# Layer 0: key squares summed with a 32-column selector as the stationary side, four token tiles in four column groups, roots on rows of tokens

## The chip, the cores and the metric

The kernel runs on one core of one Trainium2 chip, as one program launch. Its time is the device time of that core in microseconds (us). A core has five engines that work side by side, each on a queue of its own: PE (TensorE, matrix products; its weight loads are listed as PEld), DVE (VectorE), ACT (ScalarE), POOL (GpSimd) and SP (SyncE, which here issues the DMAs). They wait for one another through semaphores. Three runs of the kernel before took 1411.02, 1413.55 and 1410.15 us, a median of 1411.02 us.

## The reference, cut to what matters

The reference is one step of a streaming encoder with two layers. A layer is a norm, a projection, a token mixer beside a memory attention, a gate, an output projection and a residual. There are 512 prompt tokens and 32 sample tokens, which the kernel treats as 544 columns of one row. Layer 0 mixes tokens with RWKV-7, with 24 heads of 64 channels. The change lies in two normalisations of that mixer:

```python
kk = k * k_k.reshape(RW_HEADS, RW_HD)
kk = kk / maximum(norm(kk, axis=-1, keepdims=True), 1e-12)        # per token and head: the key norm
k  = k * (1.0 + (a - 1.0) * k_a.reshape(RW_HEADS, RW_HD))
def step(S, inp):                                                 # over the tokens
    r_t, k_t, v_t, w_t, kk_t, a_t = inp
    sa = einsum('bhvk,bhk->bhv', S, -kk_t)
    S = S * w_t[:, :, None, :] + sa[..., None] * (kk_t * a_t)[:, :, None, :] + v_t[..., None] * k_t[:, :, None, :]
    return S, einsum('bhvk,bhk->bhv', S, r_t)
S_T, y = lax.scan(step, S0, xs)
mean = mean(y, axis=-1); var = mean(square(y - mean), axis=-1)
y = (y - mean) * rsqrt(var + GN_EPS) * ln_w + ln_b                # per token and head: the output norm
y = y + sum(r * k * r_k, axis=-1, keepdims=True) * v
```

Both need a reciprocal square root for each token and head: 544 x 2 roots for a pair of heads for the keys, and as many for the outputs.

## The kernel before, in words

Layer 0 goes through 12 pairs of heads, 128 channels on the 128 partitions. What belongs to a pair is cut into kinds of work, each a Python generator whose steps are recorded one at a time by `go(kind, pr)`:

- "prep" (`rw_prep`) makes the operands of a pair from its projected rows. It squares the keys (`sq`), sums the squares over the 64 channels of a head on PE (`ps_ss`), clips the sums into `q20`, makes decays (`ps_wa`, `th`, `cum`, `de`), and later multiplies the keys by the roots: the roots are split into a high and a rest part (`rr`), transposed on PE (`ps_rt`), copied by ACT (`r4`, in the profile r<-ps_rt) and spread over the channels by a product with the selector `hs4` (`ps_b`).
- "chain" (`chunk`) is the recurrence itself, nine chunks of tokens and three hops for each: `ps_c<-SB,zr` then `avz` on DVE, `ps_c<-avz,at` then `sv` on ACT, `ps_c<-sv,bt` then `SB` on DVE. Each hop waits for the engine before it.
- "mrg" (`rw_merge`) builds the triangular inverses of a pair with small products, in two of its steps `ps_w<-t1b,at` (t1b is a transpose on DVE) and `ps_w<-at,wm`.
- "fin" (`rw_finish`) is the output norm of the pair before: mean, squares, sums into the other half of `q20`, `yt` times the root on DVE, five transposes on PE (`ps_y`), two DVE operations that read them (`bv<-ps_y`), and the gate.
- "rsq" takes the roots of all 20 columns of `q20` at once into `r20` (in the profile both are called q), by eight DVE operations on 128x20 elements, a start value from the bits and two iterations. Those on `nt` belong to it.

Token tiles lie on partitions for these roots: `ps_ss` has one column for each head and each of five token tiles, made by five products with `sq` as the stationary side and the selector `hsel` (128x2) as the moving side.

All the rest of PE's time goes to the large projections `ps_g`. Each weight block is loaded by DMA (raw) and split into a high part by ACT (`whi`) and a rest by DVE (`wlo`). One `ps_g` pass streams 272 columns. They form one endless generator, `main`, and fill every place between the small products.

The order is fixed by the program. Every PE, DVE and ACT instruction goes through `tie`, which makes it follow the one before it on its engine; therefore all of them carry line 104 in the profile (105 after the change). For each pair a table `PLAN` of 23 steps sets what is recorded: a step is one hop of the chain, then two halves, each a list of (kind, pair offset, PE us, DVE us). The last two numbers are costs by hand: `took` and `load` add them up and give each half a due time, up to which `next(main)` adds `ps_g` passes. `some(room)` puts the splits of weight blocks (`wlo`, `whi`) where DVE's sum has room. Pairs 0 to 2 are prepared ahead by `FILL0` to `FILL3` with "rsq" behind their third prep step; pair `pr` prepares pair `pr`+3 and finishes pair `pr`-1 for `pr` = 1 to 8.

Two tile pools in PSUM matter: `psm` with several buffers (tag "m"), and `psx` with one buffer:

```python
self.psx = self.pool("psx", 1, space=PS)
```

`ps_w` of "mrg", the first four transposes of `ps_y`, `ps_yc` and `ps_rt` all come from `psx`. Whoever writes there next waits until the last reader of the one before is done; for `ps_y` that is the first DVE operation `bv<-ps_y`.

Of the kernel before, what the change touches and what calls it, by code (L numbers as in the profile page):

```python
# [31 lines left out]
GN_EPS = 64e-5  # L32
KAPPA = 0.5 * math.exp(-0.5)
QB, KB = 2, 1
RKV = 4
# [13 lines left out]
    [[("val", 0, 0.95, 0), ("prep", 2, 0.1, 0)], [("prep", 2, 0, 0.42)]],  # L49
# [57 lines left out]
class Trunk:  # L107
# [20 lines left out]

    def rsqrt(self, y, x, pool, tag):

        nc = self.nc
        t = pool.tile(list(y.shape), F32, tag=tag, name=tag)
        f = 0.375 ** 0.2
        self.ve.tensor_scalar(y.bitcast(I32), x.bitcast(I32), -0.5, float(0x5F3759DF), ALU.mult, ALU.add)
        self.ve.scalar_tensor_tensor(t[:], y, -0.5 * f, y, ALU.mult, ALU.mult)
        self.ve.tensor_tensor(t[:], t[:], x, ALU.mult)
        self.ve.scalar_tensor_tensor(y, t[:], 1.5 * f, y, ALU.add, ALU.mult)
        self.ve.tensor_tensor(t[:], y, y, ALU.mult)
        self.ve.tensor_tensor(t[:], t[:], x, ALU.mult)
# [2044 lines left out]
```

## Time and profile before

| what | value |
|---|---|
| median of 3 runs | 1411.02 us (1410.15 to 1413.55) |
| the profiled execution, its span | 1409.44 us, 1407.5 us |
| PE busy | 1368.6 us, 97% of the span |
| DVE, ACT, POOL busy | 932.4, 823.9, 374.7 us (66%, 59%, 27%) |
| layer 0's pairs with prep and fin (`pr` = 1 to 8) | about 46.1 us each, from 180 us to 550 us |

A busy share says how long an engine worked, not whether the end hung on it. PE works 97% of the span, so each idle stretch of PE is short, and a row in the timeline names it and what ended it in brackets. Products on PE overlap: a `ps_g` pass is shown with 0.29 us but the next begins 0.125 us after it, so the price of a product is read from the distance of the starts. A float32 product counts as two passes, so x10 in the timeline are five `ps_ss` products, and x32 are the 16 small products of `ps_w`.

### The profile page before, as it was taken

The page shows a single profiled execution, that of the slowest core. Times are in us where ns is not written, and L with a number is a line of the kernel's source. Part 1 is how long each engine was busy: PE and PEld are TensorE (multiplying, and loading weights), DVE is VectorE, ACT ScalarE, POOL GpSimd, SP SyncE. Part 2 cuts the span into 40 slices and gives each one's busy share as a digit, 9 for nine tenths or more (in the row PEclk, how much of TensorE's full clock was granted, in tenths as well). Part 3 has the DMA queues.
Part 4 walks back from the last instruction along what each step waited for, and adds up shares of the span by engine and source line. Part 5 has one row for each costly group of instructions (what it writes and reads, how often), then busy time and mean ns, then how long its engine had stood idle before and what let it go on. Part 6 is the DMA issues. An engine that isn't in the chain of part 4 may idle for free.

```text
span 1407.5 us, 31863 instructions
## 1 busy us (share of the span) xinstructions
PE 1368.6 (97%) x11877; PEld 1304.7 (93%) x11877; DVE 932.4 (66%) x2345; ACT 823.9 (59%) x2282; POOL 374.7 (27%) x838
## 2 busy tenths in 40 slices
PE   8999999999999999999999999999999999999997
PEld 6998899999999998898899999999999999999997
DVE  5676777777877887676753466666466756667443
ACT  5765677767786777555543356664466546665222
POOL 2137558655765577510000040000000001001100
PEclk9999999999999999999999999999999999999999
DMA  7543222332233222342464473333333323332321
GB/s 222 155 118 82 61 56 65 80 98 60 67 81 94 67 73 73 95 119 77 130 182 130 131 200 104 91 92 93 98 91 93 103 73 84 93 103 89 91 76 72
DMA packets 264036, 139.45 MB, mean 99 GB/s; under 512 B 57721, under 2 KB 252802, under 8 KB 263882
## 3 DMA queue, kind: packets, MB, share of 16 engines
q1 hardware_dynamic: 263818, 137.41, 34.6%
q8 instruction: 94, 1.54, 0.5%
q14 instruction: 60, 0.49, 0.1%
q10 hardware_dynamic: 64, 0.02, 0.0%
HBM read 111.12 MB, written 22.91 MB: 95 GB/s over the span
## 4 chain that ended last, share of the span: by engine, by line
PE 78%; DVE 9%; ACT 8%; issue 2%; DMA 1%; SPq 1%; DVEq 0%; ACTq 0%
PE ps_g L104 54%; PE ps_c L104 4%; PE ps_at L104 2%; PE ps_o L104 2%; ACT pt L104 2%; PE ps_s L104 2%; DVE wlo L104 2%; PE ps_v L104 1%; ACT whi L104 1%; PE ps_mm L104 1%; PE ps_mo L104 1%; PE ps_ss L104 1%; PE ps_yc L104 1%; PE ps_w L104 1%; ACT kh L104 1%
## 5 line engine op out<-in xcount | busy, mean ns | idle before, releaser
L104 PE MATMUL ps_g<-hh,wlo 128*128 128x272 f32 x1808 | 537.2, 298 | 2.4 <-DVE wlo L104 2.4
L104 PE MATMUL ps_g<-hh,whi 128*128 128x272 f32 x1808 | 537.6, 298 | 0.4 <-DVE memk L104 0.2
L104 PE MATMUL ps_g<-hl,whi 128*128 128x272 f32 x1808 | 533.0, 296 | 0.6 <-DVE hl L104 0.3
L104 PEld LDWEIGHTS ps_g<-hh,wlo 128*128 128x128 f32 x1808 | 340.9, 189 | 8.0 <-DVE wlo L104 3.5
L104 PEld LDWEIGHTS ps_g<-hh,whi 128*128 128x128 f32 x1808 | 341.6, 189 | 5.1 <-DVE og L104 0.6
L104 PEld LDWEIGHTS ps_g<-hl,whi 128*128 128x128 f32 x1808 | 340.9, 189 | 4.7 <-DVE hl L104 1.3
L104 DVE TENSOR_TENSOR wlo<-raw,whi 128x512 fp32r<-128x512 f32 x314 | 219.0, 708 | 124.0 <-ACT whi L104 119.2
L104 ACT CAST whi<-raw 128x512 fp32r<-128x512 f32 x314 | 189.6, 617 | 108.1 <-PE ps_g L104 60.2
L851 POOL TENSOR_TENSOR tm<-u,m 102x84 f32<-102x84 f32 (+23 forms) x341 | 148.6, 436 | 165.4 <-DMA m<-sc 139.7
L853 POOL TENSOR_TENSOR u<-u,tm 102x84 f32<-102x84 f32 (+23 forms) x341 | 146.3, 429 | 26.7
L104 PE MATMUL ps_g<-hi,whi 128*128 128x272 f32 x512 | 148.9, 291 | 0.0
L104 PE MATMUL ps_g<-hi,wlo 128*128 128x272 f32 x512 | 147.8, 289 | 0.4 <-DVE wlo L104 0.4
L104 PE MATMUL ps_g<-lo,whi 128*128 128x272 f32 x512 | 147.7, 288 | 0.0
L1305 POOL TENSOR_TENSOR lo<-og,hi 128x544 fp32r<-128x544 f32 x8 | 13.2, 1648 | 462.0 <-ACT hi L104 461.5
L104 PEld LDWEIGHTS ps_g<-hi,wlo 128*128 128x128 f32 x512 | 96.4, 188 | 0.6 <-DVE wlo L104 0.6
L104 PEld LDWEIGHTS ps_g<-lo,whi 128*128 128x128 f32 x512 | 96.4, 188 | 0.0
L104 PEld LDWEIGHTS ps_g<-hi,whi 128*128 128x128 f32 x512 | 96.4, 188 | 0.0
L104 ACT ACTIVATE pt<-ps_s,snm 128x128 f32<-128x128 f32 (+3 forms) x96 | 50.9, 532 | 42.1 <-DVE snm L104 41.8
L104 DVE SCALAR_TENSOR_TENSOR SB<-ps_c,dl,sd 64x64 f32<-64x64 f32 x168 | 47.5, 283 | 42.4 <-PE ps_c L104 38.9
L1724 POOL TENSOR_TENSOR hl<-hn,hh 128x544 fp32r<-128x544 f32 x8 | 12.7, 1590 | 210.5 <-ACT hh L104 210.4
L104 ACT COPY sv<-ps_c 64x64 f32<-64x64 f32 x192 | 39.5, 206 | 44.4 <-PE ps_c L104 42.5
L104 ACT ACTIVATE sg<-ps_g 128x272 f32<-128x272 f32 x64 | 25.3, 395 | 58.1 <-PE ps_g L104 53.6
(388 smaller groups left out, 2583.2 us busy)
## 6 DMA issues: line engine op xcount, KB each, us to landing
raw<-in_rw_in_dram SPq DMA_DIRECT2D x114, 256.0 KB
raw<-in_df_in_dram SPq DMA_DIRECT2D x112, 256.0 KB
raw<-in_w_out_dram SPq DMA_DIRECT2D x64, 256.0 KB
oscr<-sg SPq DMA_DIRECT2D x16, 272.0 KB
lo<-oscr SPq DMA_DIRECT2D x16, 272.0 KB
m<-sc SPq DMA_DIRECT2D x33, 128.0 KB
raw<-in_w_mem_v_dram SPq DMA_DIRECT2D x16, 256.0 KB
kh<-kh SPq DMA_DIRECT2D x24, 136.0 KB
```

What stands on the lines that cost most here:

```text
L104: return lambda *a, **k: self.trunk.tie(self, issue(*a, **k))
L851: nc.gpsimd.tensor_tensor(tm[:, :n, :wd], u3[:, :n, kx : kx + 1].to_broadcast(sh), m3[:, kx : kx + 1, kx + 1 :].to_broadcast(sh), ALU.mult)
L853: nc.gpsimd.tensor_tensor(u3[:, :n, kx + 1 :], u3[:, :n, kx + 1 :], tm[:, :n, :wd], ALU.add)
L1305: (self.nc.gpsimd if g % 2 and self.o1 else self.ve).tensor_tensor(lo[:], t, hi[:].bitcast(F32), ALU.subtract)
L1724: nc.gpsimd.tensor_tensor(self.hl[:, k, :], h[:], self.hh[:, k, :].bitcast(F32), ALU.subtract)
```

## The change

- `hsel` becomes the stationary side with 32 columns (head 0 in the even, head 1 in the odd ones), and `sq` the moving side. Four products of 32x128 write the four token tiles of the prompt to four groups of 32 rows in PSUM (`tile_position=(0, 32 * i)`), four of 32x32 write the sample tokens beside them. The sums lie on rows of tokens now, 160 columns (`NS`), each 16 times over.
- The roots are therefore taken on 128x160 or, with the 10 columns of the output norm behind them, on 128x170 (`qn`, `r20`). `newton` has the same eight operations, and can stop in the middle: "half" in `PLAN` stands for four of them. The 10 columns are now scaled in `roots` instead of in `rw_finish`.
- `ps_rt`, its DVE inputs and its ACT copy go. `rr` is the rounded root (CAST, 128x160), and `r4` is made by one more DVE operation that leaves the root in the even row pairs and the rest in the odd ones (`nlo` is a column of 0 and -1, made once). `hs4` is built for these rows.
- `PLAN` changes in its last seven steps: "rsq" becomes two "half", and the steps of "fin" that use the roots, `yt` and `ps_y` with `bv<-ps_y`, and the gate, stand half a step to one step later. The costs by hand change too, and with them the places of the `ps_g` passes.

The diff, cut to its core (a few rows of `PLAN` and of the constants are left out):

```diff
-    [[("prep", 3, 1.04, 0.17)], [("mrg", 1, 0, 0.86)]],
-    [[("mrg", 1, 0.9, 0)], [("rsq", 0, 0, 1.5)]],
-    [[("prep", 3, 0.33, 0)], [("fin", -1, 0, 0.88)]],
-    [[("prep", 3, 0.33, 0)], [("prep", 3, 0, 0.1), ("fin", -1, 0.6, 1.0)]],
-    [[("prep", 3, 0.33, 0)], [("mrg", 1, 0.9, 0), ("prep", 3, 0.33, 0), ("fin", -1, 0, 0.73)]],
-    [[("prep", 3, 0, 1.45), ("val", 1, 0.45, 0)], [("prep", 3, 0, 0.5)]],
-    [[("out", 0, 1.6, 0.7)], [("prep", 3, 0, 0)]]]
+    [[("prep", 3, 0.52, 0.35)], [("mrg", 1, 0, 0.86)]],
+    [[("mrg", 1, 0.9, 0)], [("half", 0, 0, 1.5)]],
+    [[("prep", 3, 0.33, 0)], [("half", 0, 0, 1.4)]],
+    [[("prep", 3, 0.33, 0), ("fin", -1, 0, 0.88)], [("prep", 3, 0, 0.1)]],
+    [[("prep", 3, 0.33, 0), ("fin", -1, 0.6, 1.0)], [("mrg", 1, 0.9, 0), ("prep", 3, 0.33, 0)]],
+    [[("prep", 3, 0, 1.45), ("val", 1, 0.45, 0)], [("fin", -1, 0, 0.73), ("prep", 3, 0, 0)]],
+    [[("out", 0, 1.6, 0.7)], [("prep", 3, 0, 0.7)]]]
...
 
+    def roots(self):
+
+        c = slice(0 if self.qn is not None else NS, NS + 10 if self.gs is not None else NS)
+        if self.qn is None:
+            self.qn = self.rk0.tile([P, 2, NS + 10], F32, tag="gsq", name="qn", bufs=1)
+        q, t = self.qn[:, 0, c], self.qn[:, 1, c]
+        if self.gs is not None:
+            self.ve.tensor_scalar(self.qn[:, 0, NS:], self.gs[:], 1.0 / 64, GN_EPS, ALU.mult, ALU.add)
+        self.qn = self.gs = None
+        yield from self.newton(self.r20[:, c], q, t)
+
     def rsqrt(self, y, x, pool, tag):
 
-        nc = self.nc
-        t = pool.tile(list(y.shape), F32, tag=tag, name=tag)
+        for _ in self.newton(y, x, pool.tile(list(y.shape), F32, tag=tag, name=tag)[:]):
+            pass
+
+    def newton(self, y, x, t):
+
         f = 0.375 ** 0.2
         self.ve.tensor_scalar(y.bitcast(I32), x.bitcast(I32), -0.5, float(0x5F3759DF), ALU.mult, ALU.add)
-        self.ve.scalar_tensor_tensor(t[:], y, -0.5 * f, y, ALU.mult, ALU.mult)
-        self.ve.tensor_tensor(t[:], t[:], x, ALU.mult)
-        self.ve.scalar_tensor_tensor(y, t[:], 1.5 * f, y, ALU.add, ALU.mult)
-        self.ve.tensor_tensor(t[:], y, y, ALU.mult)
-        self.ve.tensor_tensor(t[:], t[:], x, ALU.mult)
-        self.ve.scalar_tensor_tensor(t[:], t[:], -10.0 / 3.0 * f ** 2, t[:], ALU.add, ALU.mult)
-        self.ve.scalar_tensor_tensor(y, t[:], 5.0 * f ** 4, y, ALU.add, ALU.mult)
+        self.ve.scalar_tensor_tensor(t, y, -0.5 * f, y, ALU.mult, ALU.mult)
+        self.ve.tensor_tensor(t, t, x, ALU.mult)
+        self.ve.scalar_tensor_tensor(y, t, 1.5 * f, y, ALU.add, ALU.mult)
+        yield
+        self.ve.tensor_tensor(t, y, y, ALU.mult)
+        self.ve.tensor_tensor(t, t, x, ALU.mult)
+        self.ve.scalar_tensor_tensor(t, t, -10.0 / 3.0 * f ** 2, t, ALU.add, ALU.mult)
+        self.ve.scalar_tensor_tensor(y, t, 5.0 * f ** 4, y, ALU.add, ALU.mult)
 
     def params(self, p, name, rows, queue=None):
 
...
-        self.hsel = c.tile([P, 2], F32, name="hsel")
+        self.hsel = c.tile([P, 32], F32, name="hsel")
-        nc.gpsimd.memset(self.hsel[:64, 0:1], 1.0)
-        nc.gpsimd.memset(self.hsel[64:, 1:2], 1.0)
+        nc.gpsimd.memset(self.hsel[:64, 0:32:2], 1.0)
+        nc.gpsimd.memset(self.hsel[64:, 1:32:2], 1.0)
-        self.hs4 = c.tile([P, 5, P], F32R, name="hs4")
+        self.hs4 = c.tile([P, 4, P], F32R, name="hs4")
-        self.ve.scalar_tensor_tensor(self.hs4[:], t4[:], 10.0, t5[:], ALU.is_equal, ALU.add)
+        self.ve.scalar_tensor_tensor(self.hs4[:], t4[:], 2.0, t5[:], ALU.is_equal, ALU.add)
+        self.nlo = c.tile([P, 1], F32, name="nlo")
+        self.ve.tensor_reduce(self.nlo[:], t5[:].rearrange("p i c -> p (i c)"), AX.X, ALU.max)
+        self.ve.tensor_scalar(self.nlo[:], self.nlo[:], -1.0, None, ALU.add)
...
         pss = self.psm.tile([P, 512], F32, tag="m", name="ps_ss")
-        for i in range(5):
-            c = min(i * P, T - P)
-            self.te.matmul(pss[:, 2 * i : 2 * i + 2], sq[:, c : c + P], self.hsel[:], start=True, stop=True)
-        self.ve.tensor_scalar(self.q20[:, :10], pss[:, :10], 1e-24, None, ALU.max)
+        for o, c, d in ((0, 0, P), (P, TP, 0)):
+            for i in range(4):
+                n = P if o == 0 else TS
+                self.te.matmul(pss[32 * i : 32 * i + 32, o : o + n], self.hsel[:], sq[:, c + i * d : c + i * d + n],
+                               start=True, stop=True, tile_position=(0, 32 * i))
+        self.qn = self.rk0.tile([P, 2, NS + 10], F32, tag="gsq", name="qn", bufs=1)
+        self.ve.tensor_scalar(self.qn[:, 0, :NS], pss[:, :NS], 1e-24, None, ALU.max)
...
         yield
-        rr = self.rr
-        self.ve.tensor_copy(rr[:, :10], self.r20[:, :10])
-        self.ve.tensor_tensor(rr[:, 10:20], self.r20[:, :10], rr[:, :10].bitcast(F32), ALU.subtract)
-        yield
         de = p.tile([P, CW], F32, tag="de", name="de", bufs=1)
         di = cum
         self.ae.activation(de[:, :CU], cum[:, :CU], AF.Exp, scale=-KAPPA)
         self.ae.activation(di[:, :CU], cum[:, :CU], AF.Exp, scale=KAPPA)
         yield
-        pst = self.psx.tile([P, 512], F32, tag="x", name="ps_rt")
-        self.te.transpose(pst[:, :P], rr[:].bitcast(F32), self.ident[:])
-        r4 = p.tile([P, P], F32R, tag="uh", name="r4", bufs=1)
-        self.ae.copy(r4[:], pst[:, :P])
+        rr = self.rr
+        self.ve.tensor_copy(rr[:], self.r20[:, :NS])
+        r4 = p.tile([P, NS], F32R, tag="uh", name="r4", bufs=1)
+        self.ve.scalar_tensor_tensor(r4[:], rr[:].bitcast(F32), self.nlo[:], self.r20[:, :NS], ALU.mult, ALU.add)
+        yield
         yield
...
-                self.te.matmul(psb[:, i % 4 * P : i % 4 * P + m], self.hs4[:, i, :], r4[:, P - m :], start=True, stop=True)
+                self.te.matmul(psb[:, i % 4 * P : i % 4 * P + m], self.hs4[:, i % 4, :], r4[:, i // 4 * P : i // 4 * P + m], start=True, stop=True)
...
         self.ve.tensor_reduce(s[:], sq[:], AX.X, ALU.add)
-        self.ve.tensor_scalar(self.q20[:, 10:], s[:], 1.0 / 64, GN_EPS, ALU.mult, ALU.add)
-        yield
-        self.ve.tensor_tensor(y, y, self.r20[:, 10:].unsqueeze(2).to_broadcast(sh), ALU.mult)
+        self.gs = s
+        yield
+        self.ve.tensor_tensor(y, y, self.r20[:, NS:].unsqueeze(2).to_broadcast(sh), ALU.mult)
...
                 if kind == "rsq":
-                    self.rsqrt(self.r20[:], self.q20[:], self.rk0, "nt20")
+                    for _ in self.roots():
+                        pass
+                elif kind == "half":
+                    if self.root is None:
+                        self.root = self.roots()
+                        next(self.root)
+                    else:
+                        next(self.root, None)
+                        self.root = None
                 elif 0 <= pr < NPAIR:
```

How this moves instructions, as they stand in the two programs. First PE around `ps_ss` in the pair `pr` = 2 (the hop `ps_c<-sv,bt` stands above it). Before:

```order
L104 MATMUL ps_c<-sv,bt 128x128
L104 MATMUL ps_ss<-hsel,sq 128x2 x5
L104 MATMUL ps_g<-hh,wlo 128x272
L104 MATMUL ps_g<-hh,whi 128x272
L104 MATMUL ps_g<-hl,whi 128x272
L104 MATMUL ps_g<-hh,wlo 128x272
L104 MATMUL ps_g<-hh,whi 128x272
L104 MATMUL ps_c<-SB_536,zr_1678 128x128
L104 MATMUL ps_w_3930<-t1b,at_89 32x32 x16
```

After:

```order
L105 MATMUL ps_ss<-sq,hsel 32x128 x4
L105 MATMUL ps_ss<-sq,hsel 32x32 x4
L105 MATMUL ps_g<-hh,wlo 128x272
L105 MATMUL ps_g<-hh,whi 128x272
L105 MATMUL ps_g<-hl,whi 128x272
L105 MATMUL ps_g<-hh,wlo 128x272
L105 MATMUL ps_g<-hh,whi 128x272
L105 MATMUL ps_g<-hl,whi 128x272
L105 MATMUL ps_g<-hh,wlo 128x272
L105 MATMUL ps_g<-hh,whi 128x272
L105 MATMUL ps_g<-hl,whi 128x272
L105 MATMUL ps_c<-SB_538,zr_1678 128x128
```

The five products have become eight, and nine `ps_g` passes instead of five stand between them and the next hop.

Second PE in the same pair, three to four steps of `PLAN` further, where `ps_y` (fin) and `ps_w<-at,wm` (mrg) stand; both write the one buffer of `psx`. Before:

```order
L104 MATMUL ps_g<-hh,wlo 128x272
L104 MATMUL ps_y<-ident,yt_101 128x128 x5
L104 MATMUL ps_g<-hh,whi 128x272
L104 MATMUL ps_g<-hl,whi 128x272
L104 MATMUL ps_g<-hh,wlo 128x272
L104 MATMUL ps_c<-SB_537,zr_1678 128x128
L104 MATMUL ps_wa<-lora_575,uh 128x272
L104 MATMUL ps_wa<-lora_575,uz 128x272
L104 MATMUL ps_g<-hh,whi 128x272
L104 MATMUL ps_g<-hl,whi 128x272
L104 MATMUL ps_g<-hh,wlo 128x272
L104 MATMUL ps_w_4028<-at_89,wm 32x32 x16
```

After:

```order
L105 MATMUL ps_g<-hh,wlo 128x272
L105 MATMUL ps_c<-SB_539,zr_1678 128x128
L105 MATMUL ps_wa<-lora_575,uh 128x272
L105 MATMUL ps_wa<-lora_575,uz 128x272
L105 MATMUL ps_y<-ident,yt_100 128x128 x5
L105 MATMUL ps_w_4034<-at_89,wm 32x32 x16
L105 MATMUL ps_wa<-lora_575,uh 128x272
L105 MATMUL ps_wa<-lora_575,uz 128x272
L105 MATMUL ps_c<-avz,at_1685 128x128
```

Three `ps_g` passes, a hop and two `ps_wa`, and three more `ps_g` passes lay between `ps_y` and `ps_w`. Now `ps_w` stands directly behind `ps_y`, and the passes stand ahead of both.

Third DVE in the same stretch, from the middle of the roots on (`q` and `nt` before, `r` and `qn` after). Before:

```order
L104 SCALAR_TENSOR_TENSOR q_100<-nt_3950,q_100 128x20
L104 TENSOR_TENSOR nt_3950<-q_100 128x20
L104 TENSOR_TENSOR nt_3950<-nt_3950,q_99 128x20
L104 SCALAR_TENSOR_TENSOR nt_3950<-nt_3950 128x20
L104 SCALAR_TENSOR_TENSOR q_100<-nt_3950,q_100 128x20
L104 TENSOR_TENSOR wlo<-raw,whi 128x512
L104 TENSOR_TENSOR yt_101<-yt_101,q_100 128x640
L104 SCALAR_TENSOR_TENSOR SB_537<-ps_c,dl,sd 64x64 x2
L104 TENSOR_TENSOR wlo<-raw,whi 128x512
L104 MEMSET cum 128x9
L104 SCALAR_TENSOR_TENSOR bv_95<-ps_y,PA,bv_95 128x512
L104 SCALAR_TENSOR_TENSOR bv_95<-ps_y,PA,bv_95 128x32
```

After:

```order
L105 SCALAR_TENSOR_TENSOR r_99<-qn,r_99 128x170
L105 TENSOR_TENSOR wlo<-raw,whi 128x512
L105 TENSOR_TENSOR qn<-r_99 128x170
L105 TENSOR_TENSOR qn<-qn 128x170
L105 SCALAR_TENSOR_TENSOR qn<-qn 128x170
L105 SCALAR_TENSOR_TENSOR r_99<-qn,r_99 128x170
L105 SCALAR_TENSOR_TENSOR SB_539<-ps_c,dl,sd 64x64 x2
L105 TENSOR_TENSOR yt_100<-yt_100,r_99 128x640
L105 MEMSET cum 128x9
L105 TENSOR_TENSOR wlo<-raw,whi 128x512
L105 TENSOR_TENSOR avz<-ps_c,avz 64x128
L105 SCALAR_TENSOR_TENSOR bv_95<-ps_y,PA,bv_95 128x512
```

A `wlo` stands between the halves, and of the others the hop's `SB` and `yt` have changed places; a `wlo` and `avz` stand between `yt` and `bv<-ps_y`.

More of the change, by code (lines that the diff above doesn't have):

```diff
@@ L24 @@
 TH = T // 2
+NS = P + TS
 MIXW = 1536
@@ L48 @@
 PLAN = [
-    [[("val", 0, 0.95, 0), ("prep", 2, 0.1, 0)], [("prep", 2, 0, 0.42)]],
+    [[("val", 0, 0.95, 0), ("prep", 2, 0, 0)], [("prep", 2, 0, 0.42)]],
     [[], [("prep", 2, 0, 1.04)]],
@@ L249, in consts_rwkv @@
             nc.gpsimd.memset(t[:], 0.0)
-        nc.gpsimd.memset(self.q20[:], 1.0)
         nc.gpsimd.memset(self.uz[:].bitcast(F32), 0.0)
-        nc.gpsimd.memset(self.rr[:].bitcast(F32), 0.0)
     def pads(self, t):
@@ L1418, in layer0 @@
             self.uz = self.rp.tile([P, 2, P], F32R, name="uz")
-            self.rr = self.rp.tile([P, P], F32R, name="rr")
+            self.rr = self.rp.tile([P, NS], F32R, name="rr")
             self.raw0 = [self.rp.tile([P, T + 1], F32, name=f"raw0{i}") for i in range(2)]
@@ L2141, in run @@
         self.rk0 = self.pool("rwk", 1, ctx=self.kctx, side="right")
-        self.q20, self.r20 = (self.rk0.tile([P, 20], F32, name=f"q20{i}") for i in range(2))
+        self.r20 = self.rk0.tile([P, NS + 10], F32, name="r20")
+        self.qn = self.gs = self.root = None
         self.yt = [self.rk0.tile([P, 5, P], F32, name="yt1")]
```

6 lines of the change are left out of this document (3 added, 3 removed).

## The prediction

> **What bounds the kernel now.** I read the page first, its busy times and the chain of waits.
>
> ```profile
> span 1407.5 us, 31863 instructions
> PE 1368.6 (97%) x11877; PEld 1304.7 (93%) x11877; DVE 932.4 (66%) x2345; ACT 823.9 (59%) x2282; POOL 374.7 (27%) x838
> PE 78%; DVE 9%; ACT 8%; issue 2%; DMA 1%; SPq 1%; DVEq 0%; ACTq 0%
> ```
>
> PE is busy 97% of the span and carries 78% of the chain that ended last. A microsecond of PE work taken away is a microsecond gained, if PE doesn't wait for it elsewhere. Then I read the stretches of single pairs: `pr` = 0 and `pr` = 2, the second like all from 1 to 8 (columns: window, length, busy PE, PEld, DVE, ACT, POOL, granted clock, DMA share, GB/s).
>
> ```profile
> 134.00:180.64 46.64, 43.26 (x447) 39.40 (x444) 30.64 (x78) 32.25 (x93) 28.98 (x75) 0.96 0.28 72
> 226.68:272.86 46.18, 45.73 (x468) 43.01 (x468) 36.21 (x90) 33.27 (x96) 30.13 (x67) 1.00 0.29 76
> ```
>
> In a steady pair PE idles 0.45 us of 46.18 (46.18 - 45.73), so there is next to nothing to win by waits and all by PE work; DVE has 10 us spare over a whole pair. The timeline shows whether it has them where the change puts work. PE in `pr` = 2, from `ps_ss` to the second `ps_w`:
>
> ```profile
> 256.16 0.39 PE L104 MATMUL ps_c<-sv,bt 128*128 128x128 f32 x2
> 256.50 1.28 PE L104 MATMUL ps_ss<-hsel,sq 128*128 128x2 f32 x10
> 257.63 0.37 PE L104 MATMUL ps_g<-hh,wlo 128*128 128x272 f32 x1
> 257.85 0.29 PE L104 MATMUL ps_g<-hh,whi 128*128 128x272 f32 x1
> ...
> 263.03 0.29 PE L104 MATMUL ps_g<-hh,wlo 128*128 128x272 f32 x1
> 263.61 0.74 PE L104 MATMUL ps_y<-ident,yt 128*128 128x128 f32 x5 [0.28 <-DVE yt L104]
> ...
> 265.29 0.28 PE L104 MATMUL ps_g<-hh,wlo 128*128 128x272 f32 x1
> 265.66 0.69 PE L104 MATMUL ps_w<-at,wm 32*32 32x32 f32 x32
> ```
>
> And DVE beside it:
>
> ```profile
> 257.81 0.17 DVE L104 TENSOR_SCALAR q<-ps_ss 128x10 f32<-128x10 f32 x1 [0.57 <-PE ps_ss L104]
> 258.01 0.90 DVE L104 STREAM_TRANSPOSE t1b<-at 32x256 f32<-32x256 f32 x2
> 258.85 0.73 DVE L104 SCALAR_TENSOR_TENSOR rkv<-raw,PA,rkv 128x544 f32<-128x544 f32 x1
> 259.61 0.30 DVE L104 TENSOR_TENSOR avz<-ps_c,avz 64x128 f32<-64x128 f32 x1
> 259.94 0.20 DVE L104 TENSOR_SCALAR q<-q 128x20 int32<-128x20 int32 x1
> ...
> 261.69 0.18 DVE L104 SCALAR_TENSOR_TENSOR q<-nt,q 128x20 f32<-128x20 f32 x1
> ...
> 262.52 0.94 DVE L104 TENSOR_TENSOR yt<-yt,q 128x640 f32<-128x640 f32 x1
> 263.49 0.58 DVE L104 SCALAR_TENSOR_TENSOR SB<-ps_c,dl,sd 64x64 f32<-64x64 f32 x2
> 264.10 0.69 DVE L104 TENSOR_TENSOR wlo<-raw,whi 128x512 fp32r<-128x512 f32 x1
> 264.85 0.91 DVE L104 SCALAR_TENSOR_TENSOR bv<-ps_y,PA,bv 128x512 f32<-128x512 f32 x2
> ```
>
> From the clipped sums to `bv` DVE hardly rests: here it is as full as PE, and PE waits twice for it, 0.28 us for `yt` at `ps_y`, and about 0.24 us at `ps_w` (265.29 + 0.125 to 265.66) for the first `bv`, since both write the one buffer of `psx`. That is nearly the pair's whole idle time. The change takes PE work out just ahead of this stretch and puts DVE work into it.
>
> **PE work removed.** Before, `ps_ss` holds PE from 256.50 to 257.63 (1.13 us), and the first pass behind it takes 0.22 (to 257.85) instead of 0.125: 1.35 us. For the new kind (fp32, 32 columns in four groups) the nearest rows are `ps_os` in layer 1:
>
> ```profile
> 949.38 0.28 PE L104 MATMUL ps_g<-hl,whi 128*128 128x272 f32 x1
> 949.59 0.43 PE L104 MATMUL ps_os<-cv,aTs 128*32 128x128 f32 x8
> 949.95 0.42 PE L104 MATMUL ps_os<-vs,aTs 32*32 32x128 f32 x8
> 950.30 0.40 PE L104 MATMUL ps_g<-hh,wlo 128*128 128x272 f32 x1
> 950.54 0.29 PE L104 MATMUL ps_g<-hh,whi 128*128 128x272 f32 x1
> ```
>
> Four products of two passes each take 0.36 us to the next block (949.59 to 949.95): they overlap, for one pass alone is 128 columns long. A second block in another tile shape takes 0.35, and the return to `ps_g` 0.24. The new block has four of 128 and four of 32 columns in one tile shape: between one such block (0.36) and two (0.71), nearer one, as the second has a quarter of the columns; I take 0.45. With the return it is 0.69, so 0.66 us saved (0.40 to 0.75) in each of 12 pairs. [...]
>
> The transpose and its copy go too.
>
> ```profile
> 271.68 0.33 PE L104 MATMUL ps_rt<-ident,rr 128*128 128x128 f32 x1
> 271.76 0.37 PE L104 MATMUL ps_g<-hh,whi 128*128 128x272 f32 x1
> ```
>
> 271.68 to 271.76 is 0.08; I take 0.06 a pair. The ACT copy is worth nothing: ACT has 13 us spare in a pair (46.18 - 33.27) and the roots are needed only steps later. The 12 pairs hold 12 x 0.72 = 8.6 us of PE work.
>
> **DVE work added.** Rows of the nearest widths (behind the first bar busy us and the mean in ns):
>
> ```profile
> L104 DVE TENSOR_TENSOR ats<-ps_ats,mk 128x128 f32<-128x128 f32 x24 | 5.9, 286 | 1.4 <-PE ps_ats L104 1.1
> L104 DVE SCALAR_TENSOR_TENSOR ssb<-ssb,srs 128x160 f32<-128x160 f32 x3 | 1.2, 384 | 0.1
> L104 DVE TENSOR_SCALAR ssb<-ssb,srs 128x160 f32<-128x160 f32 x3 | 0.9, 303 | 0.1
> ```
>
> A root has one TENSOR_SCALAR, four SCALAR_TENSOR_TENSOR and three TENSOR_TENSOR. On 170 columns I take 0.30, 0.37 and 0.32: 0.30 + 1.48 + 0.96 = 2.74 us, with the 0.03 between them 3.0, against 1.93 before (259.94 to 261.87). So +1.1, between +0.8 (were all eight 0.29) and +1.3. The clip from PSUM grows from 0.17 to about 0.3, `rr` and `r4` add 0.3 later. Together +1.5 us in a pair, of which 1.2 stand ahead of `yt`.
>
> **The steady pair, walked through.** Time 0 is the hop at 256.16. The new `ps_ss` ends at 0.34 + 0.45 = 0.8, with its drain 1.1, where DVE's clip begins (before at 1.65). Then, by the rows, from start to start where they follow each other: clip 0.3, `t1b` 0.9, `avz` 0.3, `rkv` 0.75 to 3.4; scaling 0.2 and half of the roots 1.5 to 5.1; `wlo` 0.65 to 5.75; the other half to 7.2; `SB` 0.6 to 7.8; `yt` 0.95 to 8.8. PE now has 41 passes, four hops and one `ps_w` from `ps_ss` to `ps_y`, where it had 29, three and one in 257.63 to 263.3: 0.44 less ahead, 12 x 0.125 more, and a hop at about 0.2 (256.16 to 256.50 is 0.34 with a change of shape in it), so it is there at 8.45. It waits 0.4 (before 0.28) and is through `ps_y` at 9.3. Now `ps_w` stands directly behind, where six passes, a hop and two `ps_wa` stood. It needs the `psx` buffer, and DVE has `wlo` (0.65), `avz` (0.25) and the first `bv` (0.75, as 264.85 to the release of `ps_w` at 265.66) from 8.85 on: 10.5. So PE waits about 1.2 us there instead of 0.24. Extra waits 0.1 + 0.95 against 0.72 of work saved: +0.25 us a pair (-0.3, if the roots take +0.8 and the rest is as walked, to +0.7, if `ps_ss` saves 0.40 and the roots take +1.3), 8 pairs: +2.0. What covered `bv` before, the work between `ps_y` and `ps_w`, has gone; the cost isn't DVE's load but this order.
>
> **The other pairs.** In `pr` = 9 and 10 `ps_w` also follows `ps_y` at once or almost so, without a prep to shorten; about the length of `bv` less what stood in the way, 0.5 each: +1.0. In the startup the roots of pair 1 stand ahead of a `wlo` for which PE waits already:
>
> ```profile
> 94.89 0.39 PE L104 MATMUL ps_g<-hh,wlo 128*128 128x272 f32 x1 [0.28 <-DVE wlo L104]
> ```
>
> +1.2 on DVE, less the 0.46 by which `ps_ss` ends earlier there: +0.7, set against 0.5 of PE work saved. Pair 0 has 0.4 us to spare on its `wlo`, so about +0.3, and pair 2 gains 0.5. Startup: +0.4 (-0.3 to +0.9). In `pr` = 0 PE waits for `t1b`:
>
> ```profile
> 166.74 0.24 PE L104 MATMUL ps_w<-t1b,at 32*32 32x32 f32 x2 [0.98 <-DVE t1b L104]
> 167.20 0.96 PE L104 MATMUL ps_w<-t1b,at 32*32 32x32 f32 x30 [0.22 <-DVE t1b L104]
> 163.97:167.38 3.41, 2.21 (x27) 1.91 (x28) 1.93 (x5) 1.08 (x3) 0.00 (x0) 1.00 0.44 137
> 167.38:170.79 3.41, 3.41 (x42) 3.35 (x37) 1.56 (x9) 1.44 (x6) 1.75 (x7) 0.50 0.66 181
> ```
>
> After the change `t1b` follows the clip at once (a `wlo` stood between, 0.7 us), and eight `ps_g` instead of three cover it: 1.2 us of waits go, with the shorter `ps_ss` up to 1.9; I take 1.5. Behind the waits the clock was granted at 0.50 for 3.41 us, worth about 1.6 us (near half of it); with the waits gone I give it even chances of going: -0.8.
>
> **Small things.** Two memsets fewer on POOL and two tiny DVE constants more stand in the startup, beside DMA-bound loading: nothing, and the DMA queue's order is unchanged. Layer 1 is untouched.
>
> **The sum.** +2.0 + 1.0 + 0.4 - 1.5 - 0.8 = +1.1 us against the profiled execution's own 1409.44 us (span 1407.5 and 1.9 around it): 1410.5. The median shown is 1411.02, 1.6 above that execution, so 1412.1 as a median. A change within 0.3% (4.2 us) can't be told from none here. The forecast is: no change, 1409.5 to 1415.
>
> **Rivals.**
>
> *Faster.* DVE may be quicker than I think or `ps_w` may not wait for `bv` as long. For it: PE is the bound everywhere else, and the `yt` it waits for is late by 0.1 only. Against it: `bv` alone takes 0.75, and nothing stands between `ps_y` and `ps_w` to hide it; even a root that costs nothing extra leaves `wlo`, `avz` and `bv` there. If the wait at `ps_w` stays at 0.24 the steady pairs save 8 x 0.65 = 5.2, and with startup and `pr` = 0 as above (-1.9) and `pr` = 9 and 10 at 0: 1411.0 - 7.1 = 1404.
>
> *Slower: the clock.* The rows of `pr` = 0 show half the clock after a stretch of 3.41 us with PE busy for 2.21. The new waits (0.4 and 1.2 within 2.2 us, with `ps_w` in small tiles behind) make such a stretch in each steady pair. Price: about 1.6 us each time; with the +1.1 of the sum, two of eight are still within 4.2, three (+5.9) are not; four, every second pair, give 1412.1 + 6.4 = 1418.5. Against it:
>
> ```profile
> 552.75 0.49 PE L104 MATMUL ps_c<-avz,at 128*128 128x128 f32 x2 [1.40 <-DVE avz L104]
> 549.30:552.71 3.41, 2.05 (x18) 1.85 (x16) 2.19 (x6) 3.31 (x9) 2.94 (x7) 1.00 0.02 5
> ```
>
> a wait of 1.40 left the clock at 1.00, with large products around it. [...]
>
> *The column groups don't overlap.* Eight products at two passes of 0.06 to 0.11 would take 1.3 and save nothing: +0.66 x 12 = +7.9, 1420. The `ps_os` row speaks plainly against it.
>
> **How the numbers follow.** No change 0.52; faster 0.25, mostly through a shorter wait at `ps_w`; slower 0.23: 0.13 the clock, 0.04 the groups, 0.06 a DVE stretch that is later than walked, by 0.4 us in each of eight pairs. The range, 1404.5 to 1418, reaches to just inside the two near rivals and leaves out 2 in 10.
>
> **What would show it.** After, `ps_ss` should last about 0.45 us in the timeline; `ps_w` should be marked with a wait of about 1.2 us ended by `bv`; PE's idle time in a steady pair should be near 1.5 us instead of 0.45, at a length of 46.4. A length near 45.5 means the faster rival, a granted clock under 0.97 in such a stretch the slower one. I am wrong if the wait at `ps_w` is under 0.5 or over 1.8 us.

## The result and the profile after

The kernel after took 1432.53 us (median of 4 runs, 1431.87 to 1436.55) against 1411.6 us before on the same chip: a ratio of 1.0155, 95% interval 1.0142 to 1.0168. That is 21 us slower, outside the range of 1404.5 to 1418. The profiled execution took 1432.77 us. First the page of the kernel after.

```profile
span 1430.8 us, 32020 instructions
PE 1376.2 (96%) x11937; PEld 1306.2 (91%) x11937; DVE 957.8 (67%) x2347; ACT 822.6 (57%) x2270; POOL 362.7 (25%) x836
PE 74%; DVE 10%; ACT 10%; issue 3%; DMA 2%; SPq 1%; POOL 1%; DVEq 0%; ACTq 0%; POOLq 0%
```

PE's busy time went up by 7.6 us although PE work was taken away: at a granted clock of 0.50 the same pass takes longer (0.23 us instead of 0.125, below). DVE has 25 us more, and the chain runs less over PE and more over DVE and ACT. Then the windows: two stretches of about a pair, and the stretches in which the granted clock (third column from the end) was 0.50.

```profile
470.00:517.00 47.00, 45.23 (x473) 41.97 (x471) 38.01 (x91) 33.07 (x95) 27.68 (x65) 1.00 0.29 75
370.70:420.00 49.30, 46.68 (x459) 43.12 (x459) 38.91 (x89) 32.22 (x93) 26.96 (x63) 0.93 0.28 72
132.82:139.65 6.83, 6.83 (x77) 6.42 (x77) 1.24 (x3) 3.82 (x10) 5.66 (x16) 0.50 0.70 195
221.57:224.98 3.41, 3.41 (x40) 3.07 (x39) 0.57 (x3) 2.36 (x5) 2.77 (x9) 0.50 0.75 227
364.93:368.34 3.41, 3.41 (x40) 3.07 (x38) 1.12 (x3) 2.12 (x5) 2.79 (x9) 0.50 0.74 222
412.71:419.54 6.83, 6.83 (x60) 5.92 (x61) 2.76 (x7) 4.27 (x13) 5.81 (x14) 0.50 0.42 125
559.49:562.90 3.41, 3.41 (x40) 3.07 (x38) 1.18 (x4) 2.17 (x5) 2.78 (x9) 0.50 0.79 227
603.86:607.27 3.41, 3.41 (x37) 3.29 (x32) 1.00 (x3) 1.10 (x3) 2.84 (x8) 0.50 0.05 12
655.06:661.89 6.83, 6.83 (x84) 6.18 (x83) 1.30 (x4) 2.94 (x10) 0.00 (x0) 0.50 0.11 41
```

In layer 0 behind the first 30 us these are ten windows of 3.41 us at half the clock, where the kernel before had one. At half the clock a `ps_g` pass follows the last after 0.23 us instead of 0.125, so a window loses 3.41 x (1 - 0.125/0.23) = about 1.55 us; nine more are 14 us. (By their mean clocks, 0.992 to 0.997, other runs of the kernel before had two or three windows in most cases, which is an estimate; the kernel after had mean clocks of 0.984 to 0.987 in all four.) The rest of the 23.3 us between the two spans is waits: a pair without such a window takes 47.1 us (`ps_ss` to `ps_ss`, 452.24 to 499.38) instead of 46.2, which makes 7.5 us in eight pairs, and some 2 us lie outside them. The timeline of PE in one such pair, and of DVE beside it:

```profile
499.38 0.49 PE L105 MATMUL ps_ss<-sq,hsel 128*32 128x128 f32 x16
499.80 0.39 PE L105 MATMUL ps_g<-hh,wlo 128*128 128x272 f32 x1
500.03 0.29 PE L105 MATMUL ps_g<-hh,whi 128*128 128x272 f32 x1
...
507.22 0.49 PE L105 MATMUL ps_c<-SB,zr 128*128 128x128 f32 x2 [0.52 <-DVE SB L105]
...
508.17 0.74 PE L105 MATMUL ps_y<-ident,yt 128*128 128x128 f32 x5 [0.21 <-DVE cum L105]
509.78 0.69 PE L105 MATMUL ps_w<-at,wm 32*32 32x32 f32 x32 [0.88 <-DVE bv L105]
```

```profile
500.02 0.33 DVE L105 TENSOR_SCALAR qn<-ps_ss 128x160 f32<-128x160 f32 x1
...
502.76 0.25 DVE L105 TENSOR_SCALAR r<-qn 128x170 int32<-128x170 int32 x1
...
504.87 0.43 DVE L105 TENSOR_TENSOR qn<-r 128x170 f32<-128x170 f32 x1
...
506.58 0.58 DVE L105 SCALAR_TENSOR_TENSOR SB<-ps_c,dl,sd 64x64 f32<-64x64 f32 x2
507.20 0.83 DVE L105 TENSOR_TENSOR yt<-yt,r 128x640 f32<-128x640 f32 x1
507.96 0.80 DVE L105 TENSOR_TENSOR wlo<-raw,whi 128x512 fp32r<-128x512 f32 x1
508.79 0.28 DVE L105 TENSOR_TENSOR avz<-ps_c,avz 64x128 f32<-64x128 f32 x1
508.99 0.89 DVE L105 SCALAR_TENSOR_TENSOR bv<-ps_y,PA,bv 128x512 f32<-128x512 f32 x2
```

`ps_ss` itself did what it should: 0.42 us to the next pass and 0.23 behind it, 0.65 instead of 1.35. But PE now idles 0.52 + 0.21 + 0.88 = 1.6 us within 3 us, for `SB`, `yt` and `bv`, all on DVE. And the view of one tile, `ps_y`, lists who waited for its buffer (us, times):

```profile
PE ps_w L105: 9.2, 10
```

The wait at `ps_w` comes in all of the ten pairs where `ps_w` follows `ps_y`, and is 9.2 us by itself.

### The profile page after: what moved, and what is told of

Same layout as the page of the kernel before. It is cut to its first block, busy times and chain, and to the rows that moved or that the text cites. A ratio compares the mean times of both kernels' runs of the same rounds, so it can differ in the third digit from the quotient of the medians.

```text
span 1430.8 us, 32020 instructions
## 1 busy us (share of the span) xinstructions
PE 1376.2 (96%) x11937; PEld 1306.2 (91%) x11937; DVE 957.8 (67%) x2347; ACT 822.6 (57%) x2270; POOL 362.7 (25%) x836
## 4 chain that ended last, share of the span: by engine, by line
PE 74%; DVE 10%; ACT 10%; issue 3%; DMA 2%; SPq 1%; POOL 1%; DVEq 0%; ACTq 0%; POOLq 0%
PE ps_g L105 51%; PE ps_c L105 4%; PE ps_at L105 2%; PE ps_v L105 2%; PE ps_o L105 2%; ACT pt L105 2%; PE ps_s L105 2%; ACT whi L105 2%; ACT sv L105 1%; DVE qn L105 1%; SPq L105 1%; PE ps_yc L105 1%; DVE wlo L105 1%; PE ps_mm L105 1%; PE ps_mo L105 1%
## 5 line engine op out<-in xcount | busy, mean ns | idle before, releaser
L868 POOL TENSOR_TENSOR tm<-u,m 102x84 f32<-102x84 f32 (+23 forms) x341 | 140.1, 411 | 187.9 <-DMA m<-sc 162.1
L870 POOL TENSOR_TENSOR u<-u,tm 102x84 f32<-102x84 f32 (+23 forms) x341 | 141.8, 416 | 26.6
```

What stands on the lines that cost most here:

```text
L868: nc.gpsimd.tensor_tensor(tm[:, :n, :wd], u3[:, :n, kx : kx + 1].to_broadcast(sh), m3[:, kx : kx + 1, kx + 1 :].to_broadcast(sh), ALU.mult)
L870: nc.gpsimd.tensor_tensor(u3[:, :n, kx + 1 :], u3[:, :n, kx + 1 :], tm[:, :n, :wd], ALU.add)
```

## The experiments

Theory A was that the new order did it: `ps_w` right behind `ps_y` on the one buffer of `psx` makes PE wait, and these waits take the clock. Theory B was that DVE's wide roots did it, wherever the steps stand. The first four kernels take the change apart.

**e1_y_in_psm** takes away the conflict on the buffer, and nothing else:

```diff
-            ps = (self.psm if q else self.psx).tile([P, 512], F32, tag="m" if q else "x", name="ps_y")
+            ps = self.psm.tile([P, 512], F32, tag="m", name="ps_y")
```

> The kernel after, with one edit: all five transposes of ps_y write buffers of psm, so that ps_w, which stands directly behind them, no longer needs the buffer of ps_y. Theory A (the new order: ps_w behind ps_y on the one buffer of psx makes PE wait 0.88 us a pair, and this wait together with the others trips the clock): the wait at ps_w goes to under 0.1, at most 0.3 us turn up at the next ps_wa, 4 or fewer windows of 3.41 us at half the clock remain in layer 0 instead of 10, time 1418 to 1424. Theory B (DVE's roots on 170 columns are the cause, and the waits for SB and yt trip the clock): time 1427 to 1432, 8 or more windows at half the clock.

It took 1415.25 us (ratio to before 1.0032, 1.0020 to 1.0044): 17 of the 21 us are gone, more than A expected. Three windows at half the clock are left, none in the eight steady pairs, whose length is back at 46.1 to 46.2 us but for the last (46.9). Its timeline of PE:

```profile
262.81 0.49 PE L105 MATMUL ps_c<-SB,zr 128*128 128x128 f32 x2
263.05 0.37 PE L105 MATMUL ps_wa<-lora,uh 128*128 128x272 f32 x1
263.26 0.29 PE L105 MATMUL ps_wa<-lora,uz 128*128 128x272 f32 x1
263.87 0.74 PE L105 MATMUL ps_y<-ident,yt 128*128 128x128 f32 x5 [0.32 <-DVE cum L105]
264.53 0.69 PE L105 MATMUL ps_w<-at,wm 32*32 32x32 f32 x32
265.43 0.39 PE L105 MATMUL ps_wa<-lora,uh 128*128 128x272 f32 x1 [0.20 <-DVE bv L105]
```

`ps_w` starts with `ps_y`'s end, and only 0.20 us of the wait for `bv` comes back, at the next user of `psm`. The wait for `SB` shrank too, to 0.1 us in this pair.

**e2_old_plan** is the kernel after with `PLAN` of before (all rows), so with the new `ps_ss` and the wide roots in the old order.

> The kernel after, with the table PLAN of before: new ps_ss, roots on 160 or 170 columns taken in one go at the old place, ps_y and bv at the old place with six ps_g passes, a hop and two ps_wa between ps_y and ps_w. Theory A (order): time 1403 to 1412, one to three windows at half the clock, the wait at ps_w under 0.4 us and the one at ps_y near 1.0. Theory B (DVE): SB and yt are as late or later, since the roots are not cut in two; time 1422 to 1435, seven or more windows at half the clock.

1417.09 us (1.0047, 1.0030 to 1.0064), two windows. Neither theory: the clock behaves as A says, but a pair is 0.6 to 1.2 us longer than before (0.8 on the mean), since the roots in one go are late for `ps_y`:

```profile
453.14 0.74 PE L105 MATMUL ps_y<-ident,yt 128*128 128x128 f32 x5 [1.67 <-DVE yt L105]
```

**e3_new_plan** is the reverse: the kernel before with `PLAN` of after and the narrow roots cut in two.

```diff
+                elif kind == "half":
+                    if self.root is None:
+                        self.root = self.newton(self.r20[:], self.q20[:], self.rk0, "nt20")
+                        next(self.root)
...
```

> The kernel before, with the table PLAN of after: old ps_ss, transposed roots on 20 columns as before, but the roots cut in two halves and yt, ps_y, bv and the gate half a step to a step later, ps_w directly behind ps_y. Theory A (order): the wait at ps_w stays near 0.8 us, since bv follows ps_y as before; five or more windows at half the clock, time 1418 to 1428. Theory B (DVE): one or two windows at half the clock, time 1409 to 1414.

1418.93 us, with a wide spread (1414.71 to 1421.04; 1.0052, 1.0036 to 1.0068). The wait stays as A says, with DVE's work as before:

```profile
451.27 0.71 PE L104 MATMUL ps_y<-ident,yt 128*128 128x128 f32 x5
452.72 0.69 PE L104 MATMUL ps_w<-at,wm 32*32 32x32 f32 x32 [0.73 <-DVE bv L104]
```

But there is one window only in the profiled execution, and none in a steady pair. By waits alone the order costs about 0.6 us in such a pair. The profiled execution is a fast one of the five (1416.01 us, mean clock 0.997); the three slowest have 0.993 to 0.995, so by that estimate they had more windows, and where is not on record. That it takes the wide roots beside the order, with their waits for `SB` and `yt`, to lose the clock in the steady pairs fits this one execution, but isn't shown.

**e4_ss_alone** has only the new products of `ps_ss` (with `hsel` of 32 columns), all else as before.

> The kernel before, with only the eight products of ps_ss in four column groups in place of the five; the clip still takes 10 columns of it, so the keys are normalised with other sums (the output differs), and transpose, roots and order are those of before. What the PE work is worth by itself. Both theories: ps_ss lasts 0.45 us to the next pass instead of 1.13, 0.66 us a pair; if PE's work is worth its whole length, 1403 to 1405; if the waits for DVE that stand behind it take it back, 1408 to 1411.

1405.74 us (0.9966, 0.9954 to 0.9978), 5.3 us faster, and the pair takes 45.5 us:

```profile
225.00:270.52 45.52, 44.99 (x474) 42.23 (x473) 36.55 (x91) 33.27 (x96) 28.31 (x66) 1.00 0.30 78
```

That is 0.66 us less in this pair, and 0.5 on the mean of the steady ones: PE is now earlier at `ps_w<-t1b` and waits there 0.22 us for `t1b` in each. The difference of 0.16 us makes 1.9 of the 2.6 us that are missing to 7.9 in 12 pairs. The profiled execution also has three windows, that of before one, but by their mean clocks (0.994 to 0.997 in both kernels) the other executions show no such difference.

**e5_wide_roots** prices DVE alone: the kernel before, the roots on 180 columns.

```diff
-                    self.rsqrt(self.r20[:], self.q20[:], self.rk0, "nt20")
+                    self.wide()
...
+        w = self.rk0.tile([P, 2, 9, 20], F32, tag="gsq", name="wide", bufs=1)
+        x = self.q20[:].unsqueeze(1).to_broadcast([P, 9, 20])
```

> The kernel before, with seven of the eight operations of the roots on 180 columns (the 20 that are needed, nine times over) in the old place and order; ps_ss, transpose and PLAN as before. DVE's price alone. If the width of the roots is what e2_old_plan lost against e4_ss_alone (1417.1 against 1405.7), the wait at ps_y grows from 0.2 to about 1.3 us a pair and the time is 1419 to 1424. Rival: the roots' width is half hidden and the rest of that difference came from the other wide operations (clip, rr, r4): 1412 to 1416.

1425.18 us (1.0094, 1.0079 to 1.0109), 13 us slower, a little more than the price by e2 less e4: in the old order the wide roots cost about 1.0 us a pair, nearly all of it at `ps_y`. There are four windows, one of them in a steady pair.

```profile
456.39 0.74 PE L104 MATMUL ps_y<-ident,yt 128*128 128x128 f32 x5 [1.28 <-DVE yt L104]
```

**e7_filled_wait** asks whether idling costs the clock. It fills the wait with passes that nobody needs:

```diff
                 self.te.transpose(ps[:, :P], yt[:, 4, :], self.ident[:])
+                for _ in range(7 if pr < 8 else 0):
+                    self.te.matmul(ps[:, P : P + TH], self.uz[:, 0, :], self.lora[0][:, :TH], start=True, stop=True)
```

> The kernel after, with seven useless passes of 272 columns (0.125 us each, 0.88 in all) between ps_y and ps_w in pairs 0 to 7, written to columns that nobody reads. PE does more work, in the time in which it waited. Theory A (idle time on PE trips the clock): the wait at ps_w falls under 0.2 us, the windows of half clock in the eight steady pairs go from 5 to none or one, time 1421 to 1426, below the kernel after although PE does 7 us more. Theory C (the clock falls for another reason, say the new products in four column groups or the whole load): 4 or more windows stay, time 1431 to 1437.

1426.18 us (1.0098 to before): 6.3 us less than the kernel after, with 7 us more work on PE. (The two were measured in different series; each beside the kernel before of its own series, it is +14.0 against +20.9 us.)

```profile
455.26 1.11 PE L105 MATMUL ps_y<-lora,uz 128*128 128x272 f32 x7
456.38 0.69 PE L105 MATMUL ps_w<-at,wm 32*32 32x32 f32 x32
```

The passes take exactly the place of the wait, so that a pair stays at 47.1 us, and the gain is the clock's: no window is left in the pairs filled (five in the kernel after), six remain in the startup and the last pairs (five). Four fewer at 1.55 us are 6.2 us. Theory C, which had four or more windows stay, falls. But the passes did two things at once: they took the idling away, and they put full-size products beside the small ones. Which of the two held the clock, this run doesn't tell.

**e8_fin_later** mends the order instead: the step with `ps_y` goes behind `ps_w`.

```diff
-    [[("prep", 3, 0.33, 0), ("fin", -1, 0.6, 1.0)], [("mrg", 1, 0.9, 0), ("prep", 3, 0.33, 0)]],
-    [[("prep", 3, 0, 1.45), ("val", 1, 0.45, 0)], [("fin", -1, 0, 0.73), ("prep", 3, 0, 0)]],
+    [[("prep", 3, 0.33, 0)], [("mrg", 1, 0.9, 0), ("prep", 3, 0.33, 0)]],
+    [[("fin", -1, 0.6, 1.0), ("prep", 3, 0, 1.45), ("val", 1, 0.45, 0)], [("fin", -1, 0, 0.73), ("prep", 3, 0, 0)]],
```

> The kernel after, with the step of fin that holds ps_y and bv moved in PLAN from step 20 to the start of step 21, so that ps_w no longer stands behind ps_y, and a product, two passes and a hop stand between ps_y and the next user of psx, ps_yc. DVE's order is the same. Theory A (the order on the one buffer): the wait at ps_w goes, no new one over 0.3 us comes at ps_yc, one to three windows at half the clock; time 1409 to 1415, like e1_y_in_psm or a little better. Theory B (DVE's wide roots set the pair's length whatever the order): waits over 1 us a pair turn up at ps_yc or the hops; 1418 or more.

1411.42 us (0.9995, 0.9986 to 1.0005): no difference from before can be measured, 21 us less than the kernel after, by the place of one step.

```profile
450.19 0.49 PE L105 MATMUL ps_c<-SB,zr 128*128 128x128 f32 x2 [0.71 <-DVE SB L105]
451.24 0.69 PE L105 MATMUL ps_w<-at,wm 32*32 32x32 f32 x32
452.77 0.77 PE L105 MATMUL ps_y<-ident,yt 128*128 128x128 f32 x5 [0.15 <-ACT at L105]
454.74 1.15 PE L105 MATMUL ps_yc<-sv,at 128*64 128x64 f32 x32
```

Neither `ps_w` nor `ps_yc` waits for `bv`. But PE waits for `SB` (up to 0.7 us) and, at other hops, for `avz`; the kernel before does neither in these pairs. The sums over the eight pairs (us, times, longest) show what takes back what the products save:

```profile
PE ps_c L105 <- DVE avz L105: 3.7, 9, 0.8
PE ps_c L105 <- DVE SB L105: 3.5, 7, 0.7
```

**The tries to get the rest.** Five kernels start from e8_fin_later, and none is better. e9_more_passes changes `("prep", 3, 0.52, 0.35)` to `("prep", 3, 0.05, 0.35)`:

> As e8_fin_later, and PE's cost of the ps_ss step in PLAN lowered from 0.52 to 0.05 us, which puts three more ps_g passes between ps_ss and ps_w<-t1b and takes them out behind, so that DVE has 0.3 us more for the roots ahead of the hop that waits for SB. If the wait for SB (0.1 to 0.5 us) is then covered: 0.2 to 0.4 us a pair better than e8_fin_later, 1406 to 1411. If the roots only push the wait to yt or bv: the same as e8_fin_later within 1 us.

1416.15 us (1.0028, 1.0017 to 1.0040): worse. `SB` is waited for as before, and the passes were taken from hops further on, which now wait for `sv` (the eight pairs again):

```profile
PE ps_c L105 <- ACT sv L105: 5.6, 7, 0.9
```

Its profiled execution also has five windows at half the clock, that of e8_fin_later two. e10_fill3 changes `FILL3 = [16, 0, 2, 6]` to `[26, 0, 2, 6]`:

> As e8_fin_later, with ten more ps_g passes (1.25 us) in the startup ahead of the first ps_w<-t1b of pair 0, taken from the passes of pr = 0. In all kernels with the new ps_ss PE reaches this product early, waits for t1b, whose operand comes by DMA, and one or two windows at half the clock follow at 133 us. If the idle time there trips the clock: no window before 160 us, 2 to 3.5 us less than e8_fin_later, 1408 to 1409.5. If the passes only move the wait (their own weights are late): as e8_fin_later, 1411 to 1412.

1416.01 us (1.0030). The wait for `t1b` went and stood, longer, at the next product of "mrg":

```profile
135.54 0.69 PE L105 MATMUL ps_w<-at,wm 32*32 32x32 f32 x32 [2.06 <-ACT wm L105]
```

e11_half_behind moves the second `("half", 0, 0, 1.4)` from step 18 into step 19, ahead of `("fin", -1, 0, 0.88)`:

> As e8_fin_later, with the second half of the roots one half step later in PLAN, behind the hop's SB on DVE instead of ahead of it; the work on DVE and its place before yt stay. If the wait for SB (0.1 to 0.7 us a pair in e8_fin_later) is the second half's 1.6 us ahead of it: the wait goes, 0.1 to 0.7 us a pair, 1407 to 1410. If yt and bv get later by what SB wins: 1411 to 1413, with the wait at ps_y.

1412.72 us (1.0008, 0.9999 to 1.0017), the same. `SB` is in time, and the wait stands one hop later:

```profile
449.98 0.49 PE L105 MATMUL ps_c<-avz,at 128*128 128x128 f32 x2 [0.70 <-DVE avz L105]
```

e12_both has both edits:

> Both edits of e10_fill3 and e11_half_behind. If both work and add up: 1404 to 1407, faster than the kernel before by 4 us or more, which is what is left of the 8.6 us of PE work taken away. If neither does: 1411.

1415.26 us (1.0024): it is as slow as e10_fill3. e13_act_helps gives two operations to ACT:

```diff
-        self.ve.tensor_scalar(self.qn[:, 0, :NS], pss[:, :NS], 1e-24, None, ALU.max)
+        self.ae.activation(self.qn[:, 0, :NS], pss[:, :NS], AF.Copy, bias=1e-24)
...
-        self.ve.tensor_copy(rr[:], self.r20[:, :NS])
+        self.ae.copy(rr[:], self.r20[:, :NS])
```

> As e8_fin_later, with two of the wide operations given to ACT, which has time to spare: the copy of the sums out of PSUM (1e-24 added instead of a maximum with it) and the rounded copy rr. DVE has 0.33 us less ahead of t1b and the roots and 0.27 less behind them. If the pairs are set by DVE's stretch from the sums to bv: 0.2 to 0.4 us a pair less than e8_fin_later, 1407 to 1409.5. If ACT's queue makes the sums late (it still has raw, so and rkv in line there): 1411 to 1415.

1414.77 us (1.0024, 1.0011 to 1.0036): the time of the second case, but not for its reason. ACT has the sums copied 0.88 us behind the start of `ps_ss` (DVE in e8_fin_later after 0.97), so they aren't late. What DVE saves it spends idle ahead of `avz`, for which it waits for PE's hop; e8_fin_later first, then e13_act_helps:

```profile
444.23 0.29 DVE L105 TENSOR_TENSOR avz<-ps_c,avz 64x128 f32<-64x128 f32 x1 [0.17 <-PE ps_c L105]
446.97 0.29 DVE L105 TENSOR_TENSOR avz<-ps_c,avz 64x128 f32<-64x128 f32 x1 [0.65 <-PE ps_c L105]
```

So the roots begin hardly earlier (3.48 us behind `ps_ss`, 3.54 in e8_fin_later), and PE waits for `SB` as before (0.66 us in this pair).

## Why the prediction was wrong

The step that failed is the clock. The forecast of "no change" let the half clock come only where it had been, and the rival that had it in the steady pairs got a chance of 0.13 and at most 1418.5 us. Its place and its price were right: windows of 3.41 us at about 1.55 us each behind the waits at `ps_y` and `ps_w`, five in the eight pairs. What it missed is that the same stands elsewhere: two windows in the startup and three in the pairs 9 to 11. In the sum the clock stood with -0.8 us and measured about +14, the steady pairs with +2.0 and measured +7.5, all the rest with -0.1 and measured about +2. The argument against the rival, one wait of 1.40 us that left the clock at 1.00, stood alone against the row in `pr` = 0 that spoke for it. The difference that the prediction named there, small products behind the waits, agrees with one window of e5_wide_roots (the last section); how much it weighs isn't known.

The second step is the steady pair: +0.25 us forecast, +0.97 measured. The wait at `ps_w` was found ahead, and nearly in its size: 1.2 forecast; the view marks 0.88, and counted as the walk counts, from 0.49 us behind the start of `ps_y`, it is 1.12. Its basis was a little off: of the 0.24 us read as a wait at `ps_w` before, about 0.1 comes with the change to small tiles, for in e8, where `ps_w` waits for nothing, it starts 0.22 us behind the last pass (451.02 to 451.24) instead of 0.125. The wait at `ps_y` was over-sized (0.4 against 0.21). The wait for `SB`, 0.52, was missed. The 0.3 us that the walk puts between the end of `ps_ss` and the clip is shown by no run: measured, the clip began 0.22 us behind the first pass after `ps_ss` (499.80 to 500.02) and directly behind `SB` on DVE, 0.64 us behind the start of `ps_ss`, where the walk has 0.76. The walk had `SB` done at 7.8 and PE at the hop only later; counted from the same hop (498.92), `SB` is ready at 8.3 (507.22) and PE was there at 7.8. One step of the sum was also added wrongly: 0.1 + 0.95 - 0.72 is +0.33 a pair and +2.6 in eight, not +0.25 and +2.0. And two windows in the rival give +4.3 us, just outside the 4.2 that it names. Neither changes what failed.

Right were: the products of `ps_ss` (0.69 forecast, 0.65 measured), the roots (3.0 us, measured 3.0 less the `wlo` between the halves), and the clip (0.3, measured 0.33). "Not DVE's load but this order" was half right: mending the order takes the 21 us back (e8), but the wide roots in the old order cost 11 to 13 us by themselves (e2 less e4, e5), so that the order had to change in some way. The window of `pr` = 0, given even chances, went. The startup, forecast at +0.4, has instead two windows at half the clock. With a shorter `ps_ss` PE is at `t1b` earlier, but its operand comes by DMA, so PE waits longer there (0.42 + 0.74 us; before 0.23). DVE's row names the DMA, PE's names DVE:

```profile
129.69 0.44 DVE L105 STREAM_TRANSPOSE t1b<-at 32x256 f32<-32x256 f32 x1 [1.91 <-DMA at<-sc]
131.16 0.69 PE L105 MATMUL ps_w<-t1b,at 32*32 32x32 f32 x30 [0.74 <-DVE t1b L105]
```

The parts, each beside the kernel before: PE work alone -5.3 us (e4), roots alone +13 (e5), order alone +7 to +8 (e3), the change in the old order +6 (e2), the whole +21, and with the order mended 0 (e8). The parts don't add up: the first three make about +15. That the missing 6 us are the clock, lost where several waits fall together in a pair, is likely from the nine windows more of the kernel after, but isn't shown; e5 lost it once in a steady pair without any marked wait.

## What to carry to other kernels

When a step is put off in an order written out by hand, list the buffers that it holds and who takes the next one from the same pool: here one step ahead of its neighbour instead of behind it was worth 21 us. Work taken from the bounding engine is gained only if the engine that feeds it isn't lengthened in the same stretch; a price on another engine has to be held against the slack of that stretch, not against its share of the span. And add up waits by stretches of 3.41 us, the length of the windows seen here, before calling them small: 1.6 us of idling in eight pairs and a few places beside cost about 9 us by themselves and 14 more by the clock, and useless work in the same place won 6 of them back. Look at the small products in such a stretch too, for in e5_wide_roots half the clock came once behind a window that held them and no marked wait.

## What the runs showed of the hardware

In the kernel after the granted clock was 0.50 for one or two whole windows of 3.41 us and 1.00 in the windows beside them, and the seven places lie on one grid: 655.06 - 132.82 = 522.24 us is 153 times 3.413 us, 221.57 - 132.82 is 26 times, and 412.71 - 364.93 is 14 times. None of the windows just ahead was idle: at six of the seven places PE was busy in it for 2.25 to 2.59 of 3.41 us, at the seventh for 1.49. And PE's busy share, as the profile shows it, didn't settle by itself whether half the clock followed. The first three rows are of the kernel after, the last two of e5_wide_roots:

```profile
409.30:412.71 3.41, 2.32 (x43) 1.85 (x44) 3.38 (x7) 0.61 (x2) 3.06 (x5) 1.00 0.00 0
460.50:463.91 3.41, 2.33 (x44) 1.78 (x43) 3.38 (x8) 0.99 (x3) 3.10 (x5) 1.00 0.03 5
463.91:467.32 3.41, 3.41 (x53) 3.00 (x54) 1.88 (x5) 3.27 (x9) 2.86 (x8) 1.00 0.45 127
259.56:262.97 3.41, 3.34 (x52) 2.94 (x52) 2.44 (x7) 2.42 (x9) 2.81 (x8) 1.00 0.12 29
262.97:266.38 3.41, 3.41 (x16) 3.41 (x16) 3.14 (x10) 2.17 (x8) 2.76 (x9) 0.50 0.60 172
```

The first two windows hold the waits of one pair each and are equally busy (2.32 and 2.33 us); the first is followed by half the clock (412.71 above), the second by 1.00. In e5_wide_roots half the clock came behind a window in which PE was busy for 98% and no wait is marked. What that window holds beside a hop and six `ps_g` passes is small: the old `ps_ss`, five products with two columns, and the 16 products of `ps_w` in tiles of 32x32. So in this one place half the clock came without a marked wait; that the short or small products were the cause is the author's estimate, from what the trace leaves, and isn't shown. How much idle time and how much small products did in the other places stays open, for no run changes one and keeps the other. Of the eight steady pairs of the kernel after, the waits of four were followed by half the clock and those of the other four by 1.00. A pair of 47.1 us is 13.8 windows long, so the same waits stand elsewhere on the grid from pair to pair; that this decides between them, and that it is also why the runs of one kernel spread, by 1.3 us (e2_old_plan) to 7.5 us (e13_act_helps), isn't shown.

DVE's operations aren't of one length: the fifth operation of the roots (`qn<-r` on 128x170 elements) took 0.37 to 0.47 us in the steady pairs of the kernel after. POOL was at work beside them in the pairs looked at, but no run took POOL's work away, so that POOL lengthens them isn't shown.
